# Decoder trunk on one Trainium2 core: sample attention by half of the heads in 16 steps of four samples, with the second half of the query projection among them

## The chip, the cores and the metric

The kernel runs on one core of one Trainium2 chip. The metric is device time in microseconds (us) of one execution, the median of several runs; lower is better. Everything is float32 in and out. The engines are TensorE (PE, matrix products and transposes), VectorE (DVE), ScalarE (ACT), GpSimd (POOL) and SyncE (SP), which here issues the loads.

## What is computed

A two-layer decoder trunk, run in one launch for a prompt of 256 tokens and for 8 samples of 4 tokens each, with the same weights. Model width is 1024. Layer 0 mixes tokens with gated linear attention, layer 1 with dilated sliding-window attention; every layer is half-step feed-forward, mixer, half-step feed-forward, each with a layer norm and with adaptive shift, scale and gate ("adaLN") from a conditioning vector. What matters here is the samples' attention in layer 1:

```python
for g in range(3):                       # windows 128, 512, 2048; dilations 1, 4, 16
    idx = wb + np.arange(T)[:, None] - dil * np.arange(steps + 1)[None, :]
    kg, vg = k_ctx[:, idx], v_ctx[:, idx]        # k_ctx: 2048 cached rows and the 4 new ones
    s = jnp.einsum('bthe,btjhe->bhtj', q[:, :, g], kg) * DIL_SCALE
    p, lse = masked_softmax(s, ...)
    o = jnp.einsum('bhtj,btjhe->bthe', p, vg)
# the three groups are joined by softmax over lse; then o @ w_out
```

There are 16 heads of 64 features. Each of the 8 samples has a cache of 2048 keys and 2048 values, a row of 1024 floats (4 KB) for each token. Because token t of a sample only meets rows of its own residue, the kernel needs the last 512 rows whole (for dilations 1 and 4) and, of the earlier 1536, every row whose number modulo 16 is 0 to 3.

## The kernel before

Activations live transposed in SBUF: features on the 128 partitions, 288 columns (256 of the prompt, 32 of the samples). A float32 product is made of three passes over split operands (`mm3`, lines 530 to 532): high by high, high by low, low by high. Weights come through one stream of jobs (`job_list`, class `Stream`): SP loads pieces of up to 512 KB into 11 raw buffers (`RAW_BUFS`) in the order of the list (line 144), and a raw buffer is loaded anew only when the piece in it has been freed. A weight piece is freed when ACT (line 176) and DVE (line 178) have split it into a high and a low part, for which there are four buffers each (`SPLIT_BUFS`, tags "hi" and "lo"); the pieces of adaLN weights and of the caches are freed when the PE has read them. The split of a weight job is asked for one job ahead.

The conditioning products (`ada_step`, line 449) are 16 small matmuls for each job of 1 MB, put wherever their job stands in the list; `weave` places those jobs between weight jobs. `ada_flush` (line 465) moves the result back to features on partitions by multiplying with a constant matrix `fold`; `fold_in` does the same at the start.

In layer 1 the work runs as follows. `dilated` first projects the queries: 12 weight jobs ("q", quarter of the heads hq, group g), each 48 matmuls of 288 columns for two chunks of 128 features, each followed by `rotate` (rotary encoding: four ACT copies of 32 partitions, a DVE and a POOL product, DVE sums). Then it walks through 16 steps and 5 more in which only values are left. A step x is a pair of samples (`pr = x // 4`), a group and a pair of tokens (`tp`). It takes four pieces of keys: for group 1 rows of 128 positions, for group 2 of 96, each row 4 KB whole. `keys` turns them by 32 PE transposes into PSUM (line 1315) and copies them out on ACT (line 1435) and DVE (line 1433), into buffers with the tags "hi" and "lo". `key_scores` multiplies them with `qz`, a tile of queries with zeros outside each head's place, which POOL fills by 16 small copies for each pair of samples (lines 1412 and 1416) after both `xh` and `xl`, the projection's inputs, are done with, since it lies in their memory (`scratch`). After four steps `softmax` and `weights` follow; `outputs` takes four pieces of values in a step, five steps behind the keys. Between these, `pieces(n)` puts in the prompt's attention, which is cut into 57 pieces: chunk c needs the projected queries of chunk c alone. All PE work of this part stands in one pinned order.

Afterwards the results are gathered (`po_all`, transposes at line 1580), split, and multiplied with the output projection's weights ("wob").

Of the kernel before, what the change touches and what calls it, by code (L numbers as in the profile page):

```python
# [9 lines left out]
F32 = mybir.dt.float32  # L10
# [8 lines left out]
P = 128  # L19
D = 1024  # L20
# [30 lines left out]
START = 5  # L51


def host_constants():
# [39 lines left out]
    g0 = np.zeros((P, TS, 33), np.float32)  # L94
    for tp in range(TS):
        g0[:, tp, 0] = np.where(tp < tr, NEG, 0)
        g0[:, tp, 32] = np.where(tp <= tr, 0, NEG)
    c["g0mask"] = g0
    c["tmask"] = (tr[:, None] == np.arange(TS)[None, :]).astype(np.float32)
    c["rmask"] = np.repeat((i[:, None] // 64 == np.arange(2)[None, :]).astype(np.float32)[:, :, None], TS, axis=2)  # L100
    c["ptmask"] = np.broadcast_to((np.arange(32)[None, :] % TS == np.arange(TS)[:, None]), (P, TS, 32)).astype(np.float32).copy()
    c["blkmask"] = ((i[:, None] % 32) // TS == np.arange(512)[None, :] // 64).astype(np.float32)
    sel = np.zeros((P, 4, 2, NS), np.float32)
    for r in range(P):
        bp, hf, t_ = r // 64, (r // 32) % 2, r % TS
        for pr in range(4):
            sel[r, pr, hf, TS * (2 * pr + bp) + t_] = 1
    c["selz"] = sel
    return c
# [6 lines left out]
class Stream:  # L116
# [22 lines left out]
    def load(self, v, j, k0, nk):  # L139
        if j["kind"] == "first":  # L140
            for m in range(2):
                self.nc.sync.dma_start(v[:, :, 256 * m:256 * m + 256], j["src"][:, k0:k0 + nk, m])
        else:
            self.nc.sync.dma_start(v, j["src"][:, k0:k0 + nk, :])
# [105 lines left out]
def job_list(I):  # L250
# [32 lines left out]
    steps = [(g, tp) for g in (1, 2) for tp in range(2)]  # L283
    for x in range(2 * NB + 5):
        g, tp = steps[x % 4]
        k = [cache_job(I, "cache_k", g, 2 * (x // 4) + bp, tp, ("K", g, x // 4, tp, bp)) for bp in range(2) if x < 2 * NB]
        g, tp = steps[(x - 5) % 4]
        v = [cache_job(I, "cache_v", g, 2 * ((x - 5) // 4) + bp, tp, ("V", g, (x - 5) // 4, tp, bp)) for bp in range(2) if x >= 5]
        ca += k + v
# [11 lines left out]
    jobs += weave(ffn(1, 1), adas((1, 3))[x:] + adas((1, 4)), lead=4, span=30) + adas((1, 5))[2:] + adas((1, 6))[:x]  # L301
    jobs += weave(wq, adas((1, 6))[x:] + adas((1, 7)), lead=4) + ca + wob + adas((1, 8))[2:]
# [4 lines left out]
def cache_job(I, name, g, b, tp, key):  # L307
    c = I[name][b].rearrange("s h e -> s (h e)")
# [3 lines left out]

        v = c.rearrange("(j t) f -> j t f", t=16)[0:J2]
    return dict(kind="r", key=key, src=v[:, 2 * tp:2 * tp + 2, :], nk=2, nc=D, rows=v.shape[0])


def body(tc, I, O, C, dbg=None):
# [46 lines left out]
    fold = cp.tile([P, 4, 9], F32, name="fold")  # L364
# [28 lines left out]
    with tc.tile_pool(name="init", bufs=1) as ip:  # L393
# [24 lines left out]
        G.tensor_copy(fold, ident.rearrange("p (q b) -> p q b", b=32)[:, :, 0:9])  # L418
# [1249 lines left out]
```

## Time and profile before

| | |
|---|---|
| median of 3 runs | 1584.7 us (1583.01 to 1585.74) |
| profiled execution, as timed | 1589.88 us |
| its span in the profile | 1588.1 us |
| mean granted TensorE clock | 0.979 |
| DVE busy | 929.9 us (59%) |
| ACT busy | 705.4 us (44%) |
| POOL busy | 260.8 us (16%) |
| bytes over the DMA queues | 342.72 MB, mean 216 GB/s |

The span is counted from the first instruction to the last; the timed figure has 1.8 us more around it. A group row of the profile gives line, engine, operation, result and operands, shape and count, then busy time and mean duration of one, then the idle time before it and what ended that. A busy PE is not a PE at its peak, since a matmul's pipelined duration overlaps the next one's. The window view gives busy time of each engine in a stretch, the granted clock, the mean busy share of the 16 DMA engines and the rate that they moved. The chain of waits follows the work that ended last back to the start.

### The profile page before, as it was taken

How to read it: one execution, taken by the hardware profiler on the slowest of the kernel's cores; microseconds unless marked ns; L12 is line 12 of the kernel's file. 1: busy time of each engine (PE TensorE's matmuls, PEld its weight loads, DVE VectorE, ACT ScalarE, POOL GpSimd, SP SyncE). 2: the span in 40 equal slices, each digit the busy share in tenths (PEclk: the TensorE clock that was granted, in tenths of full speed). 3: DMA queues.
4: the chain of work that ended last, by engine and by line, in shares of the span. 5: the costliest groups of instructions: out<-in, count | busy, mean ns of one | idle time of the engine just before them, and what ended most of it. 6: DMA issues, size and time to landing. Idle time of an engine off the chain costs nothing.

```text
span 1588.1 us, 31330 instructions
## 1 busy us (share of the span) xinstructions
PE 1499.7 (94%) x12564; PEld 1344.7 (85%) x12564; DVE 929.9 (59%) x1887; ACT 705.4 (44%) x1138; POOL 260.8 (16%) x408
## 2 busy tenths in 40 slices
PE   6999999999989999999999999899998988899996
PEld 4999997888869999988999999698755637899995
DVE  4544446596786444458554445666664667755556
ACT  2443333745635434336444433486333344444432
POOL 0000033102450000333000003323431112300001
PEclk9999999999999999999999999899998999999998
DMA  9966775554856677765556576675999996555520
GB/s 320 312 222 224 246 255 185 188 166 150 305 189 205 218 251 243 245 222 174 192 173 205 186 240 200 208 237 172 281 307 277 289 301 241 191 168 160 158 95 31
DMA packets 238820, 342.72 MB, mean 216 GB/s; under 512 B 12743, under 2 KB 202385, under 8 KB 238674
## 3 DMA queue, kind: packets, MB, share of 16 engines
q1 hardware_dynamic: 236210, 333.41, 65.5%
q0 software_dynamic: 2048, 7.14, 1.2%
q8 instruction: 98, 1.61, 0.4%
q14 instruction: 48, 0.39, 0.1%
q10 hardware_dynamic: 416, 0.17, 0.0%
HBM read 332.42 MB, written 8.26 MB: 215 GB/s over the span
## 4 chain that ended last, share of the span: by engine, by line
PE 79%; DVE 8%; DMA 7%; ACT 3%; issue 2%; POOL 1%; SPq 0%; DVEq 0%; ACTq 0%
PE pa L530 22%; PE pa L531 21%; PE pa L532 21%; DMA raw<-in_cache_k_dram 5%; PE pd L449 3%; PE pa L1315 2%; PE pb L1312 2%; PE pa L1312 1%; DVE xm L516 1%; PE pa L973 1%; DVE z L639 1%; DMA raw<-in_cache_v_dram 1%; DVE xl L525 1%; DVE lo L178 1%; DMA raw<-in_w_ada_dram 1%
## 5 line engine op out<-in xcount | busy, mean ns | idle before, releaser
L530 PE MATMUL pa<-xh,hi 128*128 128x288 f32 x1888 | 560.9, 301 | 11.7 <-ACT xh L523 8.4
L531 PE MATMUL pa<-xl,hi 128*128 128x288 f32 x1888 | 563.1, 299 | 2.7 <-DVE xl L525 2.5
L532 PE MATMUL pa<-xh,lo 128*128 128x288 f32 x1888 | 559.7, 297 | 3.4 <-DVE lo L178 3.4
L178 DVE TENSOR_TENSOR lo<-raw,hi 128x1024 fp32r<-128x1024 f32 (+1 forms) x345 | 414.8, 1211 | 228.9 <-ACT hi L176 220.7
L176 ACT ACTIVATE hi<-raw 128x1024 fp32r<-128x1024 f32 x350 | 358.6, 1035 | 254.4 <-PE pa L531 232.2
L530 PEld LDWEIGHTS pa<-xh,hi 128*128 128x128 f32 x1888 | 357.0, 191 | 25.4 <-ACT xh L523 9.4
L531 PEld LDWEIGHTS pa<-xl,hi 128*128 128x128 f32 x1888 | 359.2, 190 | 6.9 <-DVE xl L525 5.2
L532 PEld LDWEIGHTS pa<-xh,lo 128*128 128x128 f32 x1888 | 358.9, 190 | 4.6 <-DVE lo L178 4.1
L530 PE MATMUL pa<-hh,hi 128*128 128x288 f32 x704 | 209.7, 298 | 0.0
L532 PE MATMUL pa<-hh,lo 128*128 128x288 f32 x704 | 208.4, 296 | 0.0
L531 PE MATMUL pa<-hl,hi 128*128 128x288 f32 x704 | 208.1, 296 | 0.0
L810 DVE TENSOR_TENSOR sa<-pa,sa 128x288 f32<-128x288 f32 x88 | 39.6, 453 | 180.3 <-PE pa L532 174.5
L530 PEld LDWEIGHTS pa<-hh,hi 128*128 128x128 f32 x704 | 132.7, 188 | 4.3 <-issue 2.1
L532 PEld LDWEIGHTS pa<-hh,lo 128*128 128x128 f32 x704 | 132.5, 188 | 0.2
L531 PEld LDWEIGHTS pa<-hl,hi 128*128 128x128 f32 x704 | 132.4, 188 | 0.1
L811 ACT ACTIVATE hh<-sa 128x288 fp32r<-128x288 f32 x88 | 38.8, 445 | 133.9 <-DVE sa L810 131.0
L584 POOL TENSOR_TENSOR z<-z,lnpiv 128x288 f32<-128x288 f32 x6 | 4.7, 805 | 489.5 <-ACT lnpiv L579 489.5
L449 PE MATMUL pd<-raw,cT 128*32 128x256 f32 x1008 | 71.9, 389 | 5.3 <-ACT adas L455 5.3
L1315 PEld LDWEIGHTS pa<-ident,raw 128*128 128x128 f32 (+1 forms) x512 | 53.1, 146 | 27.6 <-issue 10.3
L809 ACT ACTIVATE sa<-pa 128x288 f32<-128x288 f32 x88 | 34.9, 401 | 92.9 <-PE pa L532 92.9
L1315 PE MATMUL pa<-ident,raw 128*128 128x128 f32 (+1 forms) x512 | 63.2, 274 | 11.1 <-DMA raw<-in_cache_k_dram 7.5
L1435 ACT ACTIVATE kt<-pa 128x512 f32<-128x512 f32 (+1 forms) x64 | 34.1, 541 | 74.3 <-PE pa L1315 65.9
(354 smaller groups left out, 1787.6 us busy)
## 6 DMA issues: line engine op xcount, KB each, us to landing
raw<-in_w_ffn_up_dram SPq DMA_DIRECT2D x172, 512.0 KB, 5.1
raw<-in_w_ada_dram SPq DMA_DIRECT2D x110, 512.0 KB, 5.0
raw<-in_w_ffn_down_dram SPq DMA_DIRECT2D x80, 512.0 KB, 4.7
raw<-in_cache_k_dram SPq DMA_DIRECT2D x32, 512.0 KB, 8.8
raw<-in_cache_v_dram SPq DMA_DIRECT2D x32, 512.0 KB, 9.7
raw<-in_w_in_a_dram SPq DMA_DIRECT2D x24, 512.0 KB, 4.8
raw<-in_w_q_b_dram SPq DMA_DIRECT2D x24, 512.0 KB, 4.5
raw<-in_cache_k_dram SPq DMA_DIRECT2D x32, 384.0 KB, 10.6
```

The lines of the kernel that those rows point to most:

```text
L176: self.pin("act", self.nc.scalar.activation(hv, src, AF.Copy))
L178: self.pin(low, eng.tensor_tensor(out=lo, in0=src, in1=hv.bitcast(F32), op=ALU.subtract))
L449: T.matmul(ps[32 * q:32 * q + 32, :], lhsT=cT[:, k, :], rhs=raw[kk][:, 256 * q:256 * q + 256], start=(k == 0), stop=(k == DC - 1), tile_po ...
L530: ins = [T.matmul(ps, lhsT=whi, rhs=xhi, start=first, stop=False), T.matmul(ps, lhsT=whi, rhs=xlo, start=False, stop=False), T.matmul(ps, ...
L531: T.matmul(ps, lhsT=whi, rhs=xlo, start=False, stop=False),
L532: T.matmul(ps, lhsT=wlo, rhs=xhi, start=False, stop=last)]
L809: A.activation(sa, pa[:, 0:NT], AF.Silu)
L810: V.tensor_tensor(out=sa, in0=pu[:, 0:NT], in1=sa, op=ALU.mult)
L811: A.activation(hh[:, m, :], sa, AF.Copy)
L1312: pin("pe", T.matmul(*a, **k))
L1315: pin("pe", T.transpose(*a))
L1435: A.activation(dst, pt, AF.Copy)
```

## The change

Four things are changed together.

1. A step now is half of the heads (`hh`), four samples (`bq`), a group and the two tokens `tp` and `tp + 2`. The bytes taken are the same, in other pieces. Values and group 2's keys come as rows of two runs of 2 KB; a piece is one job. Group 1's keys come as four DMAs of 128 KB, each to 32 partitions, in runs of 512 B.
2. Group 1's keys are turned on the DVE, by one instruction of 32x32 block transposes for each piece, in place of PE transposes and copies out of PSUM. Since a feature's place on the partitions then differs, the queries and the new keys are brought into the same order by small selecting matmuls (`by_fours`), and all of a step's samples use the four column groups of the PE. Group 2's keys still go through the PE, and ACT alone copies them out. The new keys' scores are made once for each four steps.
3. The second half of the query projection (6 of 12 weight jobs) is moved into the first three steps (`second_half`), two jobs in each. The first `qz` has its own tile; the queries are placed by one DVE product with a mask. Values follow four steps behind the keys. The prompt's pieces are put in three to a step in the first three steps, four afterwards.
4. The adaLN results are folded by PE transposes in place of the product with `fold`. The adaLN jobs of (1, 6) are taken in the feed-forward before, so that the query projection's list has two such jobs left of six.

The core of the diff:

```diff
-    jobs += weave(ffn(1, 1), adas((1, 3))[x:] + adas((1, 4)), lead=4, span=30) + adas((1, 5))[2:] + adas((1, 6))[:x]
-    jobs += weave(wq, adas((1, 6))[x:] + adas((1, 7)), lead=4) + ca + wob + adas((1, 8))[2:]
+    jobs += weave(ffn(1, 1), adas((1, 3))[x:] + adas((1, 4), (1, 6)), lead=4, span=30) + adas((1, 5))[2:] + adas((1, 7))[:x]
+    jobs += weave(wq[:6], adas((1, 7))[x:], lead=4) + ca + wob + adas((1, 8))[2:]
...
+    for x in range(STEPS + LAG):
+        if x < STEPS:
+            ca += [key_job(I, x, b) for b in range(4)]
+        if x < 3:
+            ca += wq[6 + 2 * x:8 + 2 * x]
+        if x >= LAG:
+            ca += [value_job(I, x - LAG, b) for b in range(4)]
...
+        elif "parts" in j:
+            for q, src in enumerate(j["parts"]):
+                dst = v[32 * q:32 * q + 32, 0, :].rearrange("p (m f) -> p m f", f=P)
+                self.nc.sync.dma_start(dst, src)
...
+def step_of(x):
+    it, j = divmod(x, 4)
+    return it // 2, it % 2, 1 + j // 2, j % 2
+
+def key_job(I, x, b):
+    hh, bq, g, tp = step_of(x)
+    c = I["cache_k"][4 * bq + b].rearrange("s h e -> s (h e)")
+    f0 = 512 * hh
+    if g == 1:
+        v = c[1536:2048, :].rearrange("(j m a) f -> a j m f", m=8, a=2)[tp]
+        return dict(kind="r", key=("K", x, b), parts=[v[:, :, f0 + P * q:f0 + P * q + P] for q in range(4)], nk=1, nc=1024)
+    v = c.rearrange("(j t) f -> j t f", t=16)[0:J2, tp:tp + 3:2, f0:f0 + 512]
+    return dict(kind="r", key=("K", x, b), src=v, nk=2, nc=512, rows=J2)
...
-            T.matmul(pf[:, 36 * h:36 * h + 36], lhsT=sb[:, P * h:P * h + P], rhs=fold, start=True, stop=True)
+            T.transpose(pf[:, P * h:P * h + P], sb[:, P * h:P * h + P], ident)
...
+        def by_fours(ps, src):
+            for e in range(4):
+                for c in range(4):
+                    mm(ps[32 * c:32 * c + 32, e], lhsT=ld["sel4"][:, e, :], rhs=src[c], start=(e == 0), stop=(e == 3),
+                       tile_position=(0, 32 * c))
...
+            V.tensor_tensor(out=qz.rearrange("p (x h t) -> p x h t", h=8, t=TS),
+                            in0=bc(qe[bq].rearrange("p x (b t) -> p (x b) t", t=TS), 2, 8),
+                            in1=bc(bc(ld["hmask"], 1, 48), 3, TS), op=ALU.mult)
...
+                if g == 1:
+                    V.transpose(out=kt.rearrange("p e (m j) -> p m e j", j=32), in_=v[0].rearrange("p k (m f e) -> p (k m) e f", e=4, f=32))
+                else:
+                    for c2 in range(2):
+                        pt = bankA().rearrange("p (f u j) -> p f u j", f=2, u=2)[:, :, :, 0:J2]
+                        for f in range(2):
+                            for u in range(2):
+                                transpose(pt[:, f, u, :], raw[u][:, 2 * c2 + f:512:4], ident[0:J2, 0:J2])
+                        A.activation(kt[:, 2 * c2:2 * c2 + 2, :].rearrange("p e (u j) -> p e u j", u=2), pt, AF.Copy)
...
+        def second_half(x):
+            hq, g = 2 + x // 3, x % 3
+            w = S.take(("q", hq, g))
+            for m in range(2):
+                p_ = bankA()
+                for k in range(DC):
+                    mm3(p_[:, 0:NT], w, m, k, xh[:, k, :], xl[:, k, :], k == 0, k == DC - 1, True)
+                rotate(p_, tab, q_out(2 * hq + m, g))
...
+        for x in range(STEPS + LAG):
             it, j = divmod(x, 4)
+            few = 1 if x < 3 else 2
+            if j == 0 and out:
+                next(out[0])
+            if x < STEPS:
                 if j == 0:
                     Sc[it] = tile("Sc", [P, 390], 2)
+                kc = keys(x)
+            pieces(few)
+            if x < 3:
+                second_half(2 * x)
+                pieces(1)
+                second_half(2 * x + 1)
+            if x == 3:
+                scratch += [pp.tile([P, DC * NT], F32, name=nm(t), tag=t, bufs=1) for t in ("xh", "xl")]
+                qz[1] = queries(1)
+            if x < STEPS:
+                key_scores(x, kc, qz[it], Sc[it])
+            if x >= LAG and j == 0:
+                out.append(outputs(it - 1, *weights(Sc[it - 1], W[it - 1])))
+            pieces(few)
             while out and next(out[0], True):
                 out.popleft()
+            if j == 2 and 0 < it < 3:
+                qz[it + 1] = queries(it + 1)
+            if x < STEPS and j == 3:
+                W[it] = softmax(it, Sc[it])
```

More of the change, by code (lines that the diff above doesn't have):

```diff
@@ L765, in fold_in @@
         def fold_in(j):
-            pf = bankB()[:, 0:36]
-            pin("pe", T.matmul(pf, lhsT=sbs[j], rhs=fold, start=True, stop=True))
+            pf = bankB()[:, 0:P]
+            pin("pe", T.transpose(pf, sbs[j], ident))
             c = slice(2 * j, 2 * j + 2)
             for m in (1, 0):
-                pin("dve", V.tensor_tensor(out=mv[:, m, c], in0=pf[:, 18 * m:18 * m + 18].rearrange("p (h b) -> p h b", h=2),
+                pin("dve", V.tensor_tensor(out=mv[:, m, c], in0=pf[:, 64 * m:64 * m + 64].rearrange("p (h b) -> p h b", h=2)[:, :, 0:9],
                                            in1=bc(bv[:, m, c], 2, 9), op=ALU.add))
@@ L1389, in dilated @@
             rotate(ps[x], tab, q_out(x % 2, x // 2))
-        for hq in range(4):
+        for hq in range(2):
             for g in range(3):
@@ new lines, in keys @@
+        def keys(x):
+            hh, bq, g, tp = step_of(x)
+            out = []
+            for b in range(4):
+                ji, v, raw = S.take(("K", x, b))
+                kt = sp.tile([P, 4, 256 if g == 1 else 2 * J2], F32, name=nm("kt"), tag=("hi", "lo")[b % 2], bufs=SPLIT_BUFS)
+                if g == 1:
[7 more added lines that the diff above has]
+                        A.activation(kt[:, 2 * c2:2 * c2 + 2, :].rearrange("p e (u j) -> p e u j", u=2), pt, AF.Copy)
+                S.free(ji)
+                out.append(kt)
+            return out
@@ L1543, in dilated @@
-        steps = [(g, tp) for g in (1, 2) for tp in range(2)]
-        qz, Sc, W = {0: queries(0)}, {}, None
-        late, out = None, deque()
-        for x in range(2 * NB + 5):
+            for j in range(4):
+                _, _, g, tp = step_of(4 * it + j)
+                rr = [S.take(("V", 4 * it + j, b)) for b in range(4)]
+                for u in range(2):
+                    t = tp + 2 * u
+                    for b in range(4):
+                        mm(po[32 * b:32 * b + 32, :], lhsT=W1[:, t, 32 * b:32 * b + 32] if g == 1 else W2[:, b, t, :],
+                           rhs=rr[b][2][u], start=(j == 0 and u == 0), stop=False, tile_position=(0, 32 * b))
+                for ji, _, _ in rr:
+                    S.free(ji)
+                if j == 3:
+                    for b in range(4):
+                        mm(po[32 * b:32 * b + 32, :], lhsT=PT[:, 32 * b:32 * b + 32], rhs=Vs[:, 512 * hh:512 * hh + 512],
+                           start=False, stop=True, tile_position=(0, 32 * b))
+                    om = tile("om", [P, 256])
+                    V.tensor_tensor(out=om, in0=po[:, 0:256], in1=ld["blkmask"][:, 0:256], op=ALU.mult)
+                yield
@@ L1555, in dilated @@
-            if late is not None:
-                key_scores(*late)
-            if 0 < x <= 2 * NB and j == 0:
-                W = softmax(it - 1, Sc[it - 1])
-            if j == 1 and it + 1 < 4:
-                qz[it + 1] = queries(it + 1)
-            pieces(x >= START)
-            if x < 2 * NB:
-                kc.append(keys(it, g, tp, 1))
-                late = (g, tp, kc, qz[it], Sc[it])
-            else:
-                late = None
-            pieces(x >= START)
-            if 4 < x <= 2 * NB + 1 and j == 1:
-                out.append(outputs(it - 1, *weights(Sc[it - 1], W)))
+                kc = keys(x)
```

212 lines of the change are left out of this document (95 added, 117 removed).

## The prediction

> **What bounds the kernel now.** I read the page's chain of waits first, for the whole run.
>
> ```profile
> PE pa L530 22%; PE pa L531 21%; PE pa L532 21%; DMA raw<-in_cache_k_dram 5%; PE pd L449 3%; PE pa L1315 2%; PE pb L1312 2%; PE pa L1312 1%; DVE xm L516 1%; PE pa L973 1%; DVE z L639 1%; DMA raw<-in_cache_v_dram 1%; DVE xl L525 1%; DVE lo L178 1%; DMA raw<-in_w_ada_dram 1%
> L530 PE MATMUL pa<-xh,hi 128*128 128x288 f32 x1888 | 560.9, 301 | 11.7 <-ACT xh L523 8.4
> L530 PE MATMUL pa<-hh,hi 128*128 128x288 f32 x704 | 209.7, 298 | 0.0
> ```
>
> The three-pass product is 64% of 1588.1 us, 1016 us. It has 3 x (1888 + 704) = 7776 matmuls, so one costs 0.131 us of the chain. Cache loads stand for 6%, and all of it lies in one place. The window view cuts out the stage that the change touches:
>
> ```profile
> 1032.00:1107.00 75.00, 74.64 (x602) 68.76 (x595) 48.66 (x120) 59.35 (x118) 20.84 (x28) 1.00 0.66 218
> 1107.00:1128.00 21.00, 18.39 (x292) 15.57 (x291) 12.50 (x37) 8.06 (x16) 12.92 (x50) 1.00 0.64 192
> 1128.00:1160.00 32.00, 31.00 (x458) 23.34 (x459) 22.09 (x74) 14.75 (x33) 10.78 (x38) 1.00 0.97 298
> 1160.00:1305.00 145.00, 129.48 (x1406) 75.77 (x1397) 86.17 (x330) 49.05 (x114) 25.88 (x75) 0.94 1.02 294
> ```
>
> The columns are length, busy us of PE, weight load, DVE, ACT, POOL, then clock, DMA share and GB/s. In the first stretch (ten of twelve query weights) the PE is full and the DMA a third idle. In the second, the DMA is still a third idle. From 1128 on the DMA engines are full and weight loads take only 76 of 145 us: this stretch lasts as long as the caches take to come. SP's waits there say the same; it waits for earlier loads to land much longer than for buffers:
>
> ```profile
> SPq L144 <- DMA raw<-in_cache_v_dram: 41.0, 42, 1.9
> SPq L144 <- DMA raw<-in_cache_k_dram: 29.4, 26, 2.1
> SPq L144 <- PE pa L1315: 22.1, 18, 4.6
> ```
>
> So two things count: when the full stretch begins and with how many pieces already asked for, and what rate it then has. PE work inside it counts only where it starves the loads.
>
> **State at 1128.** Issues from 1060 to 1128, then from 1128 to 1305:
>
> ```profile
> raw<-in_cache_k_dram SPq DMA_DIRECT2D x13, 512.0 KB, 5.5
> raw<-in_cache_k_dram SPq DMA_DIRECT2D x8, 384.0 KB, 4.4
> ```
>
> ```profile
> DMA packets 16270, 52.11 MB, mean 294 GB/s; under 512 B 1808, under 2 KB 4201, under 8 KB 16246
> raw<-in_cache_k_dram SPq DMA_DIRECT2D x19, 512.0 KB, 11.3
> ```
>
> 21 of 128 cache pieces are asked for by 1128; the other 107 take until the last values.
>
> **When the full stretch begins after the change.** The rows:
>
> ```profile
> 1088.57 1.00 PE pd L449 x16
> ```
>
> ```profile
> 1107.27 0.37 PE pb L465 x4
> ...
> 1108.56 0.82 POOL xm L1227
> ...
> 1120.26 3.41 PE pa L1315 x32
> 1123.67 3.37 PE pb L1312 x94
> ```
>
> ```profile
> 1031.74 1.07 PE L449 MATMUL pd<-raw,cT 128*32 128x256 f32 x16
> 1032.90 0.40 PE L530 MATMUL pa<-xh,hi 128*128 128x288 f32 x1
> ```
>
> The third query weight starts at 1032.9. Four jobs remain ahead of the steps: 4 x 48 x 0.131 = 25.2 us; two adaLN jobs cost 1.0 us each. That is 1060. Then the selecting matmuls wait for the last `rotate`:
>
> ```profile
> L1225 ACT ACTIVATE xm<-pa 32x288 f32<-32x288 f32 x89 | 35.8, 402 | 11.3 <-PE pa L532 5.5 <-POOL kt L1439 1.8 <-POOL xm L1227 1.8
> L1227 POOL TENSOR_TENSOR xm<-xm,ropeq 128x288 f32<-128x288 f32 x22 | 17.8, 810 | 53.9 <-ACT xm L1225 31.6 <-DVE lo L178 8.7 <-issue 8.1
> ```
>
> 4 x 0.40 + 0.81 = 2.4 us, and 48 small matmuls at the 3.37/94 of line 1312 are 1.7: start of step 0 at 1064. The mask product that makes `qz` lies under the first moved weights. POOL's copies, which hold the PE and so the loads from 1108 to 1119 now, are gone.
>
> A step of the first two holds 2 x 48 x 0.131 = 12.6 us of projection, scores 3.4 (the 94 above), three pieces of prompt work. Prompt rows from 1107 to 1311 add up to 36 us, with the smaller ones about 40, for some 50 pieces: 0.8 us each, 2.4.
>
> ```profile
> L1312 PE MATMUL pb<-KT,qT 64*128 64x256 f32 x72 | 12.0, 405 | 0.0
> L1312 PE MATMUL pb<-KT,qT 64*128 64x128 f32 x72 | 9.9, 341 | 0.5 <-DVE mx L1331 0.5
> L1315 PE MATMUL pa<-ident,pe 128*128 128x128 f32 x48 | 7.8, 299 | 0.0
> L1312 PE MATMUL pa<-pT,Vt 128*64 128x256 f32 x32 | 6.2, 417 | 1.0 <-ACT pT L1354 1.0
> ```
>
> Key tiles and weight splits share four buffers of each tag. With two of them held by keys, the second weight of a step is split only as the first one's parts come free: I add 1 us, an estimate from one ACT and one DVE pass (1.0 and 1.2 us below) less one prompt piece. So 19.4 us a step; step 2 has 32 PE transposes (3.4) and half the scores (1.8): 21.2. Together 60: step 3 starts at 1124, its first freed buffer refills at 1126. Loads asked for by then: the 12 pieces of steps 0 to 2 and the 11 buffers, 23. The loads of these steps (12.6 MB with the weights, 43 us at 294 GB/s) fit below 60.
>
> **How long the rest takes.** 105 pieces: 20 of group 1's keys and 85 others, 29 of 524 kB and 56 of 393 kB, 37.2 MB. Runs of 2 KB instead of 4 KB aren't shown; runs of 1 KB moved 380 GB/s in the full early stretch, so I cost them as now: 126.5 us at 294 GB/s.
>
> ```profile
> 28.00:40.00 12.00, 10.30 (x142) 9.29 (x144) 7.68 (x26) 3.68 (x6) 0.00 (x0) 1.00 1.09 380
> ```
>
> Group 1's keys come in 512 B runs, four DMAs of 32 partitions. Nearest rows, the first 40 us and SP's issues:
>
> ```profile
> q10 hardware_dynamic: 416, 0.17, 1.7%
> ```
>
> ```profile
> L144 SPq DMA_DIRECT2D raw<-in_cache_k_dram x64: 312/336/1487, 1075.4 to 1251.6; - x64
> ```
>
> 1.7% of 16 engines' 40 us is 10.9 us for 416 packets of 410 B, 26 ns each. A piece is 1024 packets over 16 engines: 1.7 us at least; four issues of 0.34 us with their waits say about the same. Now a piece takes 524 kB / 294 = 1.78 us. Under load the 4 KB runs reach 294 where 1 KB runs reach 380, a ratio of 1.29: 1.7 x 1.29 = 2.2 us, which I take. The upper end is half of today's rate, 3.57 us (first rival). 20 x 2.2 = 44. The last values land at 1126 + 126.5 + 44 = 1296.5 against the 1302 of now (next fence: the values' last matmuls start at 1301.75): **-5.5 us**.
>
> **The tail.** At the end of the page's timeline the PE still owes the prompt's last piece:
>
> ```profile
> 1301.75 1.92 PE L1312 MATMUL pa<-raw,xl 96*32 96x512 f32 x6
> ...
> 1305.31 0.87 PE L1315 MATMUL pa<-ident,pe 128*128 128x128 f32 x6
> 1306.50 0.65 PE L1312 MATMUL pa<-pT,Vt 128*64 128x256 f32 x2 [0.31 <-ACT pT L1354]
> 1307.82 0.86 PE L1312 MATMUL pa<-pT,Vt 128*64 128x256 f32 x6 [0.68 <-ACT pT L1354]
> 1308.62 0.64 PE L1312 MATMUL pd<-om,c_selz 128*32 128x256 f32 x8
> ```
>
> After the change 9 pieces go into three steps and 4 into each later one, so all 57 are done by step 14. That removes 1305.3 to 1308.6; the two-part mask product, now in a row, gives about 0.8 back: **-2.5 us**.
>
> **Folds and adaLN.** A fold of 4 passes costs 0.37 us (above); two transposes at 3.41/32 cost 0.21. 17 of 18 flushes lie in PE-full stages: 17 x 0.16, **-2.5 us**. The four adaLN jobs that leave the query stage cost 4 x 1.0 us in the feed-forward before it, where the PE is full too, so the stage starts 4 us later than I have reckoned; one job that stands ahead of 1032.9 now (the one at 1031.74) no longer does, since both that stay are counted behind it: **+3 us**. Should loads in that feed-forward not keep up with 4 MB more, it would cost more; its line 530 waits little for anything now.
>
> **DVE and ACT.** The block transpose isn't shown. Its nearest row moves the same 1024 elements a partition:
>
> ```profile
> L178 DVE TENSOR_TENSOR lo<-raw,hi 128x1024 fp32r<-128x1024 f32 (+1 forms) x345 | 414.8, 1211 | 228.9 <-ACT hi L176 220.7
> L176 ACT ACTIVATE hi<-raw 128x1024 fp32r<-128x1024 f32 x350 | 358.6, 1035 | 254.4 <-PE pa L531 232.2
> L1435 ACT ACTIVATE kt<-pa 128x512 f32<-128x512 f32 (+1 forms) x64 | 34.1, 541 | 74.3 <-PE pa L1315 65.9
> ```
>
> I take 1.2 us; the ends are the 0.5 us of a 512-element copy and 2.4 us, should reading every fourth element halve it. 32 of them are 39 us, about what DVE's copies out of PSUM cost now; in the full stretch DVE has 59 of 145 us free. ACT's copies of group 2 take 32 x 2 x 0.54 = 35 us, as now. Neither sets the end there.
>
> **Sum:** -5.5 - 2.5 - 2.5 + 3 = -7.5 us. The profiled execution was timed at 1589.9, 5 us over the median of 1584.7; there the sum gives 1582.4, and on the median, which is what I forecast, **1577 us**.
>
> **Rivals.**
> (a) *Half the DMA ports: slower.* A DMA to 32 partitions writes a part of SBUF's width at a time. Should the four parts of a piece go at half of 294 GB/s, a piece takes 3.57 us, 20 pieces 27 us more than I took: 1604. It decides against the change from 2.6 us a piece on (7.5 / 20 above 2.2). For it: DMAs to 96 partitions land later though smaller,
>
> ```profile
> raw<-in_cache_v_dram SPq DMA_DIRECT2D x32, 512.0 KB, 9.7
> ...
> raw<-in_cache_v_dram SPq DMA_DIRECT2D x32, 384.0 KB, 12.3
> ```
>
> against it: parts for other partitions are in flight at the same time. The Trainium skill ("SBUF — State Buffer", Door 1: The DMA port swizzle) says that the rate depends on how many of 16 ports the partitions reach, and 32 partitions reach as few as 64 do, eight; by it this rival's price holds. The landings of 96 partitions agree in sign. Chance 0.2.
> (b) *The first steps become DVE's: no change.* In steps 0 and 1 DVE has 4 block transposes, 4 low parts (9.6 us together at 1.2), 4 rotations (about 4.4) and the prompt's and scores' work, some 5.5: 19.5 against PE's 19.4. If a block transpose takes 2.4 us, the two steps take 5 us more each: 1587. Chance 0.2.
> (c) *The loads get faster.* If 2 KB runs move at 330 instead of 294 GB/s, 126.5 us become 113: 1563. For it, the 380 of 1 KB runs; against it, SP issues no more at once than now. Chance 0.13.
> The forecast itself, from 1566 to 1582, has 0.47.
>
> **Range and chances.** The low end takes (c) with group 1's pieces at their 1.7 us bound half of the way, 1563 - 5; the high end takes (a): 1558 to 1604. A measurement of this kernel can tell about 0.2%, 3 us, from no change. Faster: forecast and (c), less what lies at 1582: 0.55. Same: most of (b), 0.16. Slower: (a) and the rest of (b), 0.29.
>
> **What would show it.** Step 0's first key scores at about 1080, step 3's keys at 1124, DMA share near 1 from there to 1297; a landing of group 1's 128 KB DMAs, a piece at 2.2 us; the block transpose at 1.2 us; no prompt work behind the last values. Wrong it is if the DMA share is full but the rate falls below 270 GB/s in steps with group 1's keys (a), or if PE waits for DVE's line 178 before 1124 (b).

## The result, and the profile after

The changed kernel takes 1654.5 us (median of 4 runs, 1649.9 to 1663.4) against 1585.2 us of the kernel before beside it: a ratio of 1.0449, 95% interval 1.0385 to 1.0512. It is **slower by some 70 us**, where 7.5 us less was forecast; the time lies outside the range given. The profiled execution was timed at 1658.5 us, its span is 1656.7 us, the granted clock 0.949 (0.979 before).

Where the 68.6 us of span lie: from the first query product to the first product of the output projection the trace of before has 296.2 us (1015.4 to 1311.6), the one after 356.8 us (1021.9 to 1378.7). That stage has 60.6 of them, 6.5 come ahead of it and 1.5 behind it.

The window view of the kernel after, 40 us a row, with the columns of before (length, busy us of PE, weight load, DVE, ACT, POOL, then clock, DMA share, GB/s):

```profile
1060.00:1100.00 40.00, 29.82 (x367) 26.36 (x364) 34.47 (x83) 22.24 (x47) 8.02 (x11) 0.91 0.56 163
1100.00:1140.00 40.00, 36.67 (x335) 34.44 (x336) 19.56 (x41) 22.17 (x45) 5.30 (x7) 0.92 0.58 155
1140.00:1180.00 40.00, 25.68 (x375) 16.31 (x373) 32.96 (x100) 14.70 (x35) 6.42 (x11) 0.80 0.60 156
1180.00:1220.00 40.00, 34.54 (x481) 23.57 (x482) 22.77 (x79) 14.19 (x34) 2.49 (x4) 0.88 0.81 197
1220.00:1260.00 40.00, 26.35 (x284) 14.94 (x282) 25.06 (x57) 6.57 (x16) 2.66 (x5) 0.72 0.83 215
1260.00:1300.00 40.00, 28.79 (x327) 17.06 (x330) 23.63 (x79) 14.13 (x35) 4.82 (x8) 0.75 1.08 240
1300.00:1340.00 40.00, 32.13 (x340) 19.98 (x333) 18.60 (x53) 9.87 (x24) 2.68 (x5) 0.78 0.76 202
1340.00:1380.00 40.00, 30.71 (x276) 12.88 (x275) 10.81 (x29) 10.32 (x20) 0.00 (x0) 0.90 0.98 292
```

The same view of the kernel before, as far as its full stretch:

```profile
1060.00:1100.00 40.00, 40.00 (x329) 36.14 (x326) 23.59 (x61) 26.63 (x54) 9.41 (x13) 1.00 0.69 234
1100.00:1140.00 40.00, 37.33 (x494) 32.36 (x493) 25.91 (x75) 20.61 (x42) 19.53 (x70) 1.00 0.70 229
1140.00:1180.00 40.00, 37.55 (x499) 24.77 (x499) 25.50 (x105) 14.56 (x34) 10.29 (x36) 1.00 1.00 272
```

Read the DMA share as time in which the loads stood still: (1 - share) x 40 us. Before, that is 12.4 + 12.0 us up to 1140 and then nothing until the values end near 1305. After, it is 17.6 + 16.8 + 16.0 + 7.6 + 6.8 + 0 + 9.6 + 0.8 = 75.2 us, 51 us more. By this estimate most of the 60.6 us is time in which too few loads were under way. A smaller part is the rate: the row from 1260 has a full DMA share and moves 240 GB/s, where the full stretch of before had 294. No engine takes the loads' place as the bound: the PE is busy 26 to 37 of 40 us, DVE 33 to 34 of 40 in two rows and 11 to 25 in the others. So the question is who should have asked for the loads.

That is SP. Its waits in the changed kernel between 1128 and 1305 (the three numbers: us in total, times, longest us):

```profile
SPq L150 <- PE pa L1336: 31.1, 6, 8.8
SPq L150 <- PE pa L1339: 19.1, 17, 9.0
SPq L150 <- DVE mx L1355: 12.3, 2, 11.9
SPq L148 <- DMA raw<-in_cache_v_dram: 8.7, 7, 2.3
SPq L150 <- DVE kt L1467: 7.1, 6, 2.5
```

The prediction shows 70 us of waiting for landings in the kernel before; in the same stretch SP waited there for buffers too, 65 us in all, most of them here:

```profile
SPq L144 <- PE pa L1315: 47.0, 29, 6.8
```

So the waits for buffers have grown from 65 to some 80 us, and those for landings have fallen from 70 to 9. What has taken their place is SP's own time: summed over the trace's records, issuing takes 86 of these 177 us, 50 before. The timeline of SP, start and length of each row, waits between its issues included; line 148 issues the parts of group 1's keys, line 150 everything else:

```profile
1202.09 12.15 SPq L148 DMA_DIRECT2D raw<-in_cache_k_dram  x16
1214.34 3.90 SPq L150 DMA_DIRECT2D raw<-in_cache_v_dram  x4
1218.33 16.77 SPq L148 DMA_DIRECT2D raw<-in_cache_k_dram  x16
1235.20 7.69 SPq L150 DMA_DIRECT2D raw<-in_cache_v_dram  x4
1242.98 2.13 SPq L150 DMA_DIRECT2D raw<-in_cache_k_dram  x4
```

Four pieces of group 1's keys take 12 to 17 us to be asked for, four of group 2's 2 us. Everything behind them waits, since SP issues in one order: the values of the same step, 4 pieces, come only after the sixteen. Two steps with group 1 take SP from 1202 to 1243, 41 us for 16 pieces, where the DMA engines of before needed 16 x 1.78 = 28 us. Of these 41 us SP waits 13, most of them here, and issues for 28:

```profile
SPq L150 <- PE pa L1339: 5.9, 2, 5.7
SPq L148 <- DMA raw<-in_cache_v_dram: 4.3, 2, 2.3
```

One issue by itself, as the view of that line gives it (ns, least, median, most):

```profile
L148 SPq DMA_DIRECT2D raw<-in_cache_k_dram x128: 560/607/1799, 1037.6 to 1297.4; - x128
```

0.61 us, where the row of before that the prediction used has 0.34. The Trainium skill ("Perfetto Trace Analysis", DMA Instruction — HWDGE) says that the profiled time of such an instruction begins when its semaphores are satisfied, though a wait for a lock is in it; so the 0.61 us holds no wait for a buffer or a landing. The rows of waits, which stand apart from it, agree.

Inside a step the PE then shows a second thing, here at the tenth step's scores (`kt` times queries):

```profile
1243.30 0.62 PE L1336 MATMUL pb<-kt,xl 128*32 128x256 f32 x2
1245.18 0.62 PE L1336 MATMUL pb<-kt,xl 128*32 128x256 f32 x2 [1.27 <-DVE kt L1467]
1247.05 0.62 PE L1336 MATMUL pb<-kt,xl 128*32 128x256 f32 x2 [1.25 <-DVE kt L1467]
1248.93 4.47 PE L1336 MATMUL pb<-kt,xl 128*32 128x256 f32 x90 [1.26 <-DVE kt L1467]
...
```

It takes one sample's matmuls after each transpose, 10 us for a set of scores that needs 2.8 in step 0. That looks like the cause; e1 below was made for it, and shows that it is not.

### The profile page after: what moved, and what is told of

It is laid out like the page before. It is cut to its first block, busy times and chain, and to the rows that moved or that the text cites. A ratio compares the mean times of both kernels' runs of the same rounds, so it can differ in the third digit from the quotient of the medians.

```text
span 1656.7 us, 31617 instructions
## 1 busy us (share of the span) xinstructions
PE 1514.3 (91%) x12764; PEld 1346.0 (81%) x12764; DVE 958.3 (58%) x1871; ACT 702.5 (42%) x1144; POOL 230.6 (14%) x275
## 5 line engine op out<-in xcount | busy, mean ns | idle before, releaser
L1248 ACT ACTIVATE xm<-pa 32x288 f32<-32x288 f32 x128 | 51.4, 402 | 31.8 <-PE pa L555 12.1
L1467 DVE STREAM_TRANSPOSE kt<-raw 128x1024 f32<-128x1024 f32 x32 | 63.2, 1999 | 0.1
L1336 PE MATMUL pb<-kt,xh 128*32 128x64 f32 (+2 forms) x512 | 35.3, 385 | 21.5 <-DVE kt L1467 14.8
```

Source lines behind the costliest of these rows:

```text
L1248: A.activation(sw[d:d + 32, :], ps[32 * q:32 * q + 32, 0:NT], AF.Copy)
L1336: pin("pe", T.matmul(*a, **k))
L1467: V.transpose(out=kt.rearrange("p e (m j) -> p m e j", j=32), in_=v[0].rearrange("p k (m f e) -> p (k m) e f", e=4, f=32))
```

## The experiments

Five theories were held against each other: **A**, the order inside a step (scores in the same step as the transposes, where the kernel before had them a step later); **B**, the transposes' time on DVE; **C**, group 1's keys in small packets and four DMAs, from which **S**, the number of issues, was later taken out; **D**, steps 0 to 3, which hold prompt and projection work; and, late, **F** and **G**, the rate of the full stretch. All times are medians; the ratio is to the kernel before on the same chip, whose medians beside these runs were between 1589 and 1595 us. Rows of the table come from several chips, so where two times differ by a few us the ratios decide. In e3, e6, e7, e10, e14, e17 and e18 the keys (in e14 the values too) come in another order or choice than the attention expects, so the samples' attention there isn't the reference's: these runs give the price of loads and transposes and are no kernels to use.

| run | edit | us | ratio, 95% interval |
|---|---|---|---|
| e1_late | after; scores a step later | 1655.7 | 1.0416 (1.0366 to 1.0466) |
| e2_pe_keys | after; group 1's keys in one DMA, by PE | 1630.8 | 1.0256 (1.0204 to 1.0307) |
| e3_one_dma | after; group 1's keys in one DMA | 1624.2 | 1.0224 (1.0161 to 1.0286) |
| e4_q_first | after; all queries ahead of the steps | 1664.2 | 1.0461 (1.0407 to 1.0514) |
| e5_late_pe | e2 and e1 | 1637.7 | 1.0280 (1.0221 to 1.0339) |
| e6_late_one | e3 and e1 | 1639.8 | 1.0291 (1.0233 to 1.0349) |
| e7_run_reads | e3; transposes read neighbours | 1620.5 | 1.0168 (1.0111 to 1.0225) |
| e8_fold | before; folds by transposes | 1585.9 | 0.9947 (0.9911 to 0.9983) |
| e9_prompt_later | e2; no prompt work in steps 0 to 3 | 1620.7 | 1.0173 (1.0122 to 1.0223) |
| e10_all_three | e7; no prompt work in steps 0 to 3 | 1613.1 | 1.0134 (1.0074 to 1.0193) |
| e11_fold_queries | e8; first queries copied by DVE | 1589.1 | 0.9989 (0.9963 to 1.0015) |
| e12_halves | before; cache pieces in two DMAs | 1576.3 | 0.9905 (0.9868 to 0.9942) |
| e13_two_dmas | e9; cache pieces in two DMAs | 1615.2 | 1.0155 (1.0121 to 1.0189) |
| e14_row_halves | e13; whole rows | 1613.1 | 1.0137 (1.0100 to 1.0174) |
| e15_halves_fold | e12 and e8 | 1569.1 | 0.9867 (0.9839 to 0.9895) |
| e16_quarters | before; cache pieces in four DMAs | 1639.3 | 1.0302 (1.0275 to 1.0330) |
| e17_one_512 | e3 with 512 B runs | 1629.8 | 1.0226 (1.0150 to 1.0302) |
| e18_four_2k | e3 in four DMAs of 32 partitions | 1659.2 | 1.0417 (1.0351 to 1.0483) |

### The order inside a step

```diff
+            if late is not None:
+                key_scores(*late)
...
+            late = (x, kc, qz[it], Sc[it]) if x < STEPS else None
+            if x < 3:
+                key_scores(*late)
+                late = None
-LAG = 4
+LAG = 5
```

> The changed kernel (1654 us), but from step 3 on the scores of a step's keys are computed one step after the keys, as the kernel before did, and the values follow five steps behind instead of four. Nothing else: same DMAs, same 32x32 transposes on DVE. Theory A (the PE's fixed order waits in the same step for transposes that stand on DVE behind prompt work which itself waits for the PE; buffers come free late; the loads starve): steps from 3 on fall from about 14.5 us to 11-12 us, 30 to 50 us in all, 1605-1625 us, PE's waits for kt (27.5 us) nearly gone. Theory B (DVE's 2.0 us transposes set the steps by their busy time): less than 10 us, 1645-1660. Theory C (the 512 B runs of group 1's keys in four DMAs of 32 partitions set them): less than 10 us, and SP's waits stay as long.

1655.7 us: nothing gained. The waits of the PE shown above are not what the time hangs on. In e1 the DMA engines are full from 1260 on, and the first of these rows moves less than the 294 GB/s of before:

```profile
1260.00:1300.00 40.00, 32.85 (x417) 17.46 (x416) 26.97 (x91) 11.00 (x26) 2.53 (x5) 0.91 1.02 229
```

So the delay could still pay once the loads were faster. It was tried again on top of the two edits of the next part, e5 on e2 and e6 on e3 (same diff).

> The changed kernel with both earlier edits: group 1's keys in one DMA of 2 KB runs and by PE transposes (1630.8 us alone), and scores one step behind their keys from step 3 on (1655.7 alone). Theory A+C (the small runs were the first bound and hid what the order inside a step costs): with the runs gone the lag pays, 10 to 25 us below 1631: 1605-1620. Theory D (the loads are late because too few are asked for before the values begin at step 4, whatever the order): 1625-1640, DMA share still about 0.5 up to 1180.

> The changed kernel with group 1's keys in one DMA of 2 KB runs, turned on DVE (1624.2 us alone; keys in another order, so the attention over groups 0 and 1 isn't the reference's), and scores one step behind their keys. Theory A+C: 10 to 25 us below 1624: 1600-1614. Theory B (DVE is full where the keys are turned: 36.8 of 40 us from 1140 to 1180) or D: 1618-1630.

1637.7 against 1630.8, and 1639.8 against 1624.2: no gain either time; the medians are higher, the intervals overlap. Theory A falls.

### Group 1's keys: what they come in

e3 asks for a piece of group 1's keys at once; e2 does the same and turns them on the PE as group 2's are.

```diff
-        v = c[1536:2048, :].rearrange("(j m a) f -> a j m f", m=8, a=2)[tp]
-        return dict(kind="r", key=("K", x, b), parts=[v[:, :, f0 + P * q:f0 + P * q + P] for q in range(4)], nk=1, nc=1024)
+        v = c[1536:2048, :].rearrange("(j t) f -> j t f", t=4)[:, tp:tp + 3:2, f0:f0 + 512]
+        return dict(kind="r", key=("K", x, b), src=v, nk=2, nc=512, rows=P)
```

> The changed kernel, but a piece of group 1's keys comes in one DMA of 128 partitions with 2 KB runs in place of four DMAs of 32 partitions with 512 B runs; the 32x32 transposes on DVE stay, so the keys stand in another order than the scores take them, and the samples' attention over group 0 and 1 isn't the reference's. Theory C (the small runs and the issues set the steps): 1600-1625 us. Theories A and B: within 10 us of 1654.

> The changed kernel, but group 1's keys come in one DMA of 128 partitions with 2 KB runs and are turned by PE transposes as group 2's are (copies out of PSUM by ACT and DVE in turn); the 32x32 transposes and the 512 B runs are gone together. Theory A (waits within a step in a fixed order): the PE then waits for two copies in place of one transpose, little gain, 1640-1660 us. Theories B and C (the transposes' time, or the 512 B runs): the 63 us of DVE and the small packets go, 32 x 3.4 us more of PE come for eight group 1 steps (27 us): 1600-1625.

Both give back 24 to 30 us by the medians, and their intervals lie below that of the changed kernel; e3 does it with the DVE transposes still in place. e2's time lies between its two ranges. Three things left together in e3: small packets, three of four issues, and DMAs of 32 partitions. e17 and e18 part the packets from the other two; in e17 the 512 B runs stay, eight to a partition, in one DMA, in e18 the four DMAs of 32 partitions stay, with runs of 2 KB.

```diff
+        runs = c[1536:2048, :].rearrange("(j t) f -> j (t f)", t=4).rearrange("j (m r f) -> j m r f", r=4, f=P)[:, :, 2 * hh + tp]
...
+            self.nc.sync.dma_start(v.rearrange("p k (q f) -> p (k q) f", q=4), j["runs"])
```

```diff
+            for q in range(4):
+                self.nc.sync.dma_start(v[32 * q:32 * q + 32], j["src"][32 * q:32 * q + 32])
```

> One DMA of 128 partitions for a piece of group 1's keys, as in the kernel of 1624.2 us, but of 512 B runs, eight to a partition, 2 KB apart: as many packets as the changed kernel has, a fourth of its issues. (Other 128-feature blocks of the same rows come, so the attention isn't the reference's.) Theory S (SP's issues: 16 of them take 10-17 us of a step): 1620-1632. Theory C (the packets: 33-45 ns for 512 B where 2 KB take 106-120): 1645-1660.

> Four DMAs of 32 partitions for a piece of group 1's keys, as the changed kernel has, but of 2 KB runs (each a quarter of the partitions of the one DMA of 1624.2 us; the attention isn't the reference's). Theory S or the 32 partitions: 1645-1660. Theory C: 1620-1630.

1629.8 and 1659.2 us, beside each other on one chip. Small packets in one issue cost 6 us by the medians (the ratios of e17 and e3 are the same); four DMAs of 32 partitions with large packets cost 29 us more than e17 and 35 more than e3, as much as e3 had given back. In e18 the DMA engines aren't full, as in the changed kernel:

```profile
1180.00:1220.00 40.00, 34.44 (x484) 22.91 (x482) 23.32 (x87) 14.19 (x34) 2.48 (x4) 0.93 0.75 199
1220.00:1260.00 40.00, 26.96 (x301) 16.69 (x300) 22.70 (x48) 9.02 (x21) 2.67 (x5) 0.75 0.80 216
```

and in e17 they nearly are:

```profile
1180.00:1220.00 40.00, 33.73 (x390) 21.25 (x394) 27.52 (x83) 13.86 (x33) 2.49 (x4) 0.80 0.92 250
1220.00:1260.00 40.00, 36.29 (x524) 24.44 (x518) 23.11 (x83) 17.09 (x40) 5.03 (x9) 0.87 1.02 253
```

The issues by the view of the line, first e18, then e17:

```profile
L151 SPq DMA_DIRECT2D raw<-in_cache_k_dram x128: 560/592/1622, 1038.2 to 1295.5; - x128
```

```profile
L150 SPq DMA_DIRECT2D raw<-in_cache_k_dram x32: 540/1178/7207, 1039.2 to 1272.4; - x32
```

A piece costs SP 4 x 0.59 = 2.4 us in four issues. In that time it can ask for no more than 524 kB / 2.4 us = 218 GB/s. One issue with as many packets as the change has took 0.54 us at the least; its longer ones, up to 7.2 us, lie for the most part where the DMA engines are nearly full already (a share of 0.88 to 1.09 in the five stretches from 1147 on in which SP issues them). So it isn't SP's time as such that costs: between 1128 and 1305 issuing takes 82 us in e17 and 83 in e18.

Whether DMAs of 32 partitions cost anything by themselves is not separated from the four issues. While SP issues the sixteen parts of a step, the rows are these, first of the changed kernel, then of e18:

```profile
1202.00:1214.00 12.00, 10.73 (x211) 8.32 (x206) 9.46 (x27) 7.59 (x19) 2.49 (x4) 1.00 1.00 216
1266.00:1281.00 15.00, 10.72 (x191) 9.20 (x192) 6.26 (x24) 6.36 (x16) 1.91 (x3) 0.86 1.13 229
```

```profile
1200.00:1214.00 14.00, 11.88 (x210) 8.39 (x206) 11.02 (x32) 8.02 (x21) 2.19 (x4) 1.00 0.78 197
1216.00:1232.00 16.00, 4.87 (x30) 1.69 (x28) 13.79 (x32) 3.14 (x8) 2.47 (x4) 0.61 0.80 232
```

In the changed kernel the DMA engines are then full at a low rate; in e18, with larger packets, they have time to spare, and it takes as long. This speaks for S, the issues, and against the DMA engines. That four issues are enough without the 32 partitions shows e16 on the kernel before, with all 128 or 96 partitions in each DMA:

```diff
+        elif (j.get("key") or " ")[0] in ("K", "V"):
+            for m in range(4):
+                self.nc.sync.dma_start(v[:, :, 256 * m:256 * m + 256], j["src"][:, k0:k0 + nk, 256 * m:256 * m + 256])
```

> The kernel before with each cache piece in four DMAs of 1 KB runs in place of one of 4 KB runs (two of 2 KB: 1576.3 us). If smaller DMAs go on helping: 1565-1574. If the issues (0.34 us each) or the packets now cost: 1578-1600.

1639.3 us, 50 more and far above both ranges. SP's timeline has no gap (between 1128 and 1305 it waits 8 us in all), and the DMA engines are a quarter idle:

```profile
1187.13 7.45 SPq L145 DMA_DIRECT2D raw<-in_cache_v_dram  x16
1194.67 8.61 SPq L145 DMA_DIRECT2D raw<-in_cache_k_dram  x16
1203.39 8.29 SPq L145 DMA_DIRECT2D raw<-in_cache_v_dram  x16
```

```profile
1180.00:1220.00 40.00, 33.79 (x303) 19.52 (x302) 18.17 (x64) 11.08 (x24) 9.23 (x30) 0.89 0.76 235
```

Sixteen issues in 8.1 us are 2.0 us a piece, more than the 1.78 that a piece took from the DMA engines. Here SP alone is the bound.

### The block transposes

e7 is e3 with transposes that read 32 neighbouring elements.

```diff
-in_=v[0].rearrange("p k (m f e) -> p (k m) e f", e=4, f=32))
+in_=v[0].rearrange("p k (m e f) -> p (k m) e f", e=4, f=32))
```

> The kernel of one DMA of 2 KB runs with DVE transposes (1624.2 us), but each 32x32 transpose reads 32 neighbouring elements in place of every fourth one; the same 1024 elements a partition are written in the same order. The keys' features are then mixed up too, so the attention isn't the reference's. If the reading of every fourth element makes the 2.0 us: one transpose 1.1-1.3 us, 25 us less on DVE in all, and, by theory B, 8 to 15 us off the time: 1609-1616. If the operation itself costs two clocks an element: 2.0 us as before and 1624 +- 4.

The groups of DVE, of the changed kernel and of e7:

```profile
L1467 DVE STREAM_TRANSPOSE kt<-raw 128x1024 f32<-128x1024 f32 x32 | 63.2, 1999 | 0.1
```

```profile
L1467 DVE STREAM_TRANSPOSE kt<-raw 128x1024 f32<-128x1024 f32 x32 | 38.6, 1224 | 2.7 <-DMA raw<-in_cache_k_dram 2.7
```

2.0 us with every fourth element (in e3, from which e7 differs by this alone, too), 1.2 with neighbours: the stride makes the difference, 25 us of DVE. The time falls by 4 us by the medians, and the intervals overlap. B is a small part.

### Steps 0 to 3

e4 uses all query weights ahead of the steps; e9 and e10 take the prompt's pieces out of steps 0 to 3.

```diff
-    jobs += weave(wq[:6], adas((1, 7))[x:], lead=4) + ca
+    jobs += weave(wq, adas((1, 7))[x:], lead=4) + ca
```

```diff
-            few = 1 if x < 3 else 2
+            few = 0 if x < 4 else 2
...
-                pieces(1)
```

> The changed kernel, but all twelve query weights are used ahead of the first step, as before the change; none stands in steps 0 to 2. If mixing them into the steps were the loss (split buffers shared with key tiles, PE waits there of 7 us and steps of 23-25 us for 19.4 forecast): about 15 us less, 1635-1645. If the steps from 3 on carry the loss (theories A, B, C): 1650-1675, since steps 0 to 2 then load less in parallel with the PE.

> The kernel with group 1's keys by the PE and in 2 KB runs (1630.8 us), but with no prompt work in steps 0 to 3 (13 pieces there now); steps from 4 on hold four pieces each. Theory D (the loads stand at half of their rate until 1180 because steps 0 to 3 take 70 us for 16 key pieces and 6 weights): steps 0 to 3 are shorter by 13 pieces at 0.8 us of PE and some waits, the DMA is full 10 to 20 us earlier: 1611-1621. Rival (that work only moves: the later steps become PE's or end later behind the last values): 1628-1640.

> One DMA of 2 KB runs, transposes reading 32 neighbours (1620.5 us; the attention isn't the reference's), and no prompt work in steps 0 to 3. If the three causes add up: 10 to 20 us below 1620: 1600-1610. If steps 0 to 3 are held by something else (the second half of q): 1617-1624.

e4 took 10 us more than the changed kernel by the medians, but its ratio is only 0.0012 higher and the intervals lie over each other. So the mixing of projection and steps isn't the loss; that it gains is not shown. By the medians e9 won 10 us against e2 and e10 won 7 against e7; the intervals overlap both times. The rows of e9 and of e2 from 1140 to 1180, e2 last:

```profile
1140.00:1180.00 40.00, 35.84 (x523) 27.27 (x520) 21.52 (x84) 17.01 (x37) 3.34 (x6) 0.96 0.69 196
```

```profile
1140.00:1180.00 40.00, 36.27 (x479) 29.38 (x481) 27.40 (x110) 20.40 (x47) 7.03 (x12) 0.96 0.53 161
```

Prompt work that is done early holds back the steps that set buffers free; done later, it lies beside fuller loads. In both the PE is busy 36 of 40 us there, which fits D: these steps belong to the PE, and the loads wait for it.

### The rate of the full stretch

```diff
+        elif (j.get("key") or " ")[0] in ("K", "V"):
+            for m in range(2):
+                self.nc.sync.dma_start(v[:, :, 512 * m:512 * m + 512], j["src"][:, k0:k0 + nk, 512 * m:512 * m + 512])
```

> The kernel before, but each piece of the caches comes in two DMAs of 2 KB runs (the halves of the rows) in place of one of 4 KB runs. A 2 KB packet took 117-122 ns in the full stretches of the changed kernels, a 4 KB packet 222-226: if that is the price of the runs, 128 pieces cost 5-8% more: 9 to 14 us slower, ratio 1.005-1.009. If the packets only wait for each other and the rate is the same: 1.000 +- 0.002.

This expectation was wrong in sign: the kernel before gets **faster**, 1576.3 us, by two DMAs of 2 KB runs. Its windows:

```profile
1180.00:1220.00 40.00, 38.35 (x460) 22.31 (x458) 24.76 (x95) 16.12 (x37) 12.06 (x42) 1.00 1.04 320
1220.00:1260.00 40.00, 38.93 (x503) 25.55 (x506) 24.48 (x90) 14.41 (x32) 4.85 (x17) 1.00 1.06 318
```

About 319 GB/s against the 294 of before; with four DMAs (e16, above) it falls to 235. Does the same help the changed kernel, and does it matter that its 2 KB runs are no neighbours? e13 divides each piece of e9 into two DMAs, one for each token; e14 lets such a piece be one token's whole row.

```diff
+                self.nc.sync.dma_start(v[:, m:m + 1, :], j["src"][:, k0 + m:k0 + m + 1, :])
```

> The kernel with group 1's keys by the PE and no prompt work in steps 0 to 3 (1620.7 us; full stretch about 280 GB/s), each cache piece in two DMAs, one for each token, in place of one. Theory F (a piece as two DMAs loads faster, as the halves did in the kernel before: 13 us): 1605-1612, rate 300 GB/s and more from 1190 on. Theory G (the far-apart 2 KB runs are slow, whatever the DMA) or H (the steps hold it): 1617-1624.

> As the one before, but a piece reads one token's whole rows (two halves of 4 KB that lie together, a DMA for each half) in place of half rows of two tokens; the same bytes in all, the values stand elsewhere, so the samples' attention isn't the reference's. Theory G: 8 to 15 us less than with the half rows of two tokens, rate above 300 GB/s. Theories F and H: within 4 us of it.

1615.2 and 1613.1 us against 1620.7, with overlapping intervals: neither F nor G accounts for much. The row of e13 at 1140 says why:

```profile
1140.00:1180.00 40.00, 35.85 (x530) 27.59 (x529) 20.36 (x83) 17.86 (x38) 2.53 (x5) 1.00 0.74 220
```

At that time the DMA engines of the kernel before, and of e12 too, are full. Theory H of that expectation, the steps, is what is left; it wasn't divided further.

### The parts that help, alone

> The kernel before the change with its adaLN folds by two transposes in place of two fp32 matmuls, nothing else. The prediction's term: 17 x 0.16 us less on the full PE, 2.5 us: 1582.5 us by 1585. If the folds lie beside waits: 1584-1586.

> The kernel before with its folds by transposes (1585.9 us beside 1592.3) and, besides, the first queries' sixteen copies on DVE in place of POOL, on which the PE waits between 1108 and 1120. If that wait holds the first keys' buffers and so the loads: 3 to 8 us below the folds alone, ratio to before 0.990-0.993. If the loads come as they come: 0.994-0.996, as the folds alone.

> The kernel before with the caches in halves (1576.3 us, ratio 0.9905) and the folds by transposes (1585.9, 0.9947). If both add up: 1571-1574, ratio 0.985-0.988.

```diff
-            T.matmul(pf[:, 36 * h:36 * h + 36], lhsT=sb[:, P * h:P * h + P], rhs=fold, start=True, stop=True)
+            T.transpose(pf[:, P * h:P * h + P], sb[:, P * h:P * h + P], ident)
...
-                    G.tensor_copy(qz[64 * i:64 * i + 64, :, c, :, TS * h8:TS * h8 + TS],
+                    (V if pr == 0 else G).tensor_copy(qz[64 * i:64 * i + 64, :, c, :, TS * h8:TS * h8 + TS],
```

The folds alone (first pair of lines) gain 0.2 to 0.9% in e8. e11 has the folds too, and the copies on DVE (second pair) besides; its interval reaches over 1, above both ranges of its expectation. So the copies gain nothing, and the folds' own gain is small and not confirmed there. e15, halves and folds, takes **1569.1 us, ratio 0.9867** (0.9839 to 0.9895). It beats both kernels, by 17 to 26 us against the one before.

## Why the prediction was wrong

**The step that failed** is the price of a piece of group 1's keys, "four issues of 0.34 us with their waits say about the same [1.7 us]", and with it the premise behind the sum, that only the rate of the DMA engines sets the stretch from 1124 on. The prediction weighed a piece by packets and bytes and took SP's issue time from a row of another shape. The issues took 0.61 us each, 2.4 us a piece. Put into the sum, that alone would add 20 x (2.4 - 2.2) = 4 us; the larger error is the overlap. The sum lets the issues lie beside the loads. In the runs the values of a step stand in SP's queue behind sixteen issues of keys, a step with group 1 holds SP 10 to 17 us for its keys, waits included, and the DMA engines are not kept full. Runs e17, e18 and e3 price four DMAs for a piece in place of one: 29 to 35 us in all, over the 20 pieces of the sum 1.5 to 1.75 us a piece more. That the order in SP's queue makes this of it is argued from the rows; no run changes that order or gives the parts to a second queue. The packets were priced about right: by the trace's records those of 512 B took 33 to 41 ns on average, 2.1 to 2.6 us a piece against the 2.2 taken.

**When the full stretch begins.** Step 0 was forecast at 1064 and 4 us more, steps 0 and 1 at 19.4 us each, step 2 at 21.2, step 3's keys at 1124. In the trace the projection of step 0 begins at 1072.5, that of step 1 at 1098.7, step 2's keys come at 1120 and step 3's at 1143: 26, 21 and 23 us. The 1 us for shared split buffers was too little. One wait of the PE there, from 1091.5 to 1098.7 for a weight to be split, is 7 us by itself:

```profile
PE pa L553 <- ACT hi L182: 7.1, 1, 7.1
```

In front of it ACT stood with the prompt's softmax, which had itself waited 3.6 us for DVE. Behind it the PE's products began 0.24 us apart until 1105.8, then 0.13 again: the prediction's 0.131 us does not hold right after such a wait, some 3 us in this place.

And a full stretch did not begin with step 3. As an estimate: steps 0 to 2 ask for eight pieces each, half of them weights, 8 x 1.78 = 14 us of loads in steps of 21 to 26 us, and step 3 asks for four, 7 us; the kernel before spends 4.5 to 6.7 us on each of the steps next to its first, with four pieces each. The forecast counted the pieces but not that the steps in which values are missing must be short. In every changed version above the DMA share is 0.48 to 0.99 from 1140 to 1180 (0.99 only in e10), and only later full. Taking the prompt's work out gave 7 to 10 us of this by the medians; e10, with the three prices out that could be taken out, is still 0.7 to 1.9% slower than before. By the DMA share its loads stood still for 41 us from 1060 to 1300, those of the kernel before for 24; the difference lies in the rows from 1100 (0.50) and 1180 (0.85). **That remainder of about 20 us stays open** as to its parts. It isn't the four issues, the 512 B packets or the strided reads, which e10 has not; DMAs per piece and whole rows changed e9 little. In e13 the PE is 90% busy from 1140 to 1180 while the DMA share is 0.74, which speaks for the steps' own PE work, but no run takes that work away.

**The rate.** 126.5 us at 294 GB/s for 85 pieces could not be tested in the changed kernel, since its loads weren't full for long. In e3, where all cache pieces come in one DMA of 2 KB runs, the full row agrees with it:

```profile
1180.00:1220.00 40.00, 33.55 (x470) 22.28 (x467) 29.94 (x88) 14.95 (x36) 2.99 (x6) 0.87 1.00 298
```

Rival (c), faster loads by 2 KB runs, is true for the kernel before in two DMAs (319 GB/s, 13 us) and was worth nothing clear of noise here (e13).

**Rival (a)**, group 1's pieces too dear, had the right sign and the place, and its 27 us is near the 29 to 35 measured. Its mechanism, half of the rate, isn't shown. Its sign, a full DMA share below 270 GB/s, does appear while the sixteen parts are issued (1.00 at 216 and 1.13 at 229, above) and in the row from 1260. But e18 takes as long with DMA engines that aren't full; and packets of 512 B took 41 ns on average between 1180 and 1300, against 31 in e17 with 128 partitions in one DMA: a third more, not twice. The rule of the Trainium skill ("SBUF — State Buffer", Door 1: The DMA port swizzle) that the prediction gave beside it is neither confirmed nor refuted by that, since no run has such DMAs alone under way. By the same section 96 partitions reach all sixteen ports, so the later landings of 96, which the prediction counted for the rule, do not bear on it.

**Rival (b)**, DVE. The transpose takes 2.0 us, not 1.2: the stride, which the prediction named as the upper end, is real (e7). DVE is fullest not only in step 0 (34 of 40 us) but from 1140 to 1180 (33 of 40), where 7 transposes meet the prompt's and the softmax's work. What e7 gave back is 4 us by the medians, not the 10 forecast for this rival; the 7 us wait above has DVE in it too.

**Folds and adaLN.** The folds' 2.5 us (17 x 0.16 is 2.7) stand at the lower edge of what e8 measured (0.17 to 0.89%, 2.7 to 14 us). The stage began 6.5 us later, where +3 less the folds' part in front of it was forecast; no run divides that.

**The tail** was right in kind: no prompt work behind the last values.

```profile
1372.24 0.59 PE L1336 MATMUL pa<-raw,xl 96*32 96x512 f32 x1
1372.25 1.44 PE L1336 MATMUL pa<-Vs,PT 128*32 128x512 f32 x5
1374.21 0.62 PE L1336 MATMUL pd<-om,c_selz 128*32 128x256 f32 x2 [0.52 <-DVE mv L685]
...
1378.68 0.98 PE L553 MATMUL pa<-xh,hi 128*128 128x288 f32 x4 [0.20 <-ACT xh L1652]
```

From the end of the values at 1372.8 to the output projection pass 5.9 us; the kernel before has about 7 by its trace, so 1 us was gained for 2.5.

**That the second half of the queries belongs among the steps** is neither refuted nor shown by e4: put back in front, the kernel takes 10 us more by the medians, with intervals that lie over each other.

## What to carry to other kernels

A queue that issues DMAs has a time of its own, like an engine: multiply the issues of a stretch by the duration of one of the same shape, and set the product beside the DMA engines' time, above all where one load becomes several. Where the DMA share is below one and no engine is full, look at what the issuing engine does between its waits. And a stretch is bound by loads only from the step on in which the steps ask for more than they last; count what each step asks for, not only what is still to come.

## What the runs showed of the hardware beside that

The time of one issue on SP went with the shape of the DMA, by the medians: 0.33 us for one run to a partition, 0.42 for quarters of 1 KB, 0.54 for 128 partitions of two runs (values of the changed kernel), 0.59 for 32 partitions of two, 0.61 for 32 of eight. One issue of 128 partitions of eight runs took 0.54 us at the least, 1.18 at the median and up to 7.2 beside full DMA engines. A load divided into two DMAs of half rows moved 319 GB/s where one DMA moved 294, and in four 235: the best size lay in between. 512 B packets in one DMA kept 250 GB/s and more. A 32x32 block transpose on DVE of 1024 elements a partition took 1.22 us from neighbouring elements and 2.0 us from every fourth. Where the PE waited between short sets of matmuls, its granted clock fell to between 0.72 and 0.80 in four of the 40 us rows, and 90 score matmuls took 4.47 us where 96 took 2.83 in step 0; what that adds to the loss was not separated from what made the PE wait.
